# Expert selection of a product-key expert layer: keys by 0/1 matrix products, gated one-hots by VectorE alone, four result banks

## The chip, the cores and the metric

One core of a Trainium2 chip runs the whole program: TensorE (matmuls), VectorE (DVE), ScalarE (ACT), GpSimd (POOL) and SyncE (SP, which issues DMAs), with SBUF and PSUM between them. The metric is the device time of one execution in microseconds (us), the median of several runs.

## The reference, cut to what matters

The program computes two blocks of sequence mixers (a retention and a forgetting attention), a third mixer of stick-breaking attention and gated delta rule, and then an expert layer over 512 tokens of width 1024. Only the last is touched:

```python
q = einsum('bsd,de->bse', h, w_q).reshape(B, S, 8, 256)
s1 = einsum('bshd,hnd->bshn', q[..., :128], keys1)      # 128 keys per half
s2 = einsum('bshd,hnd->bshn', q[..., 128:], keys2)
v1, i1 = top_k(s1, 16);  v2, i2 = top_k(s2, 16)
cand = (v1[..., :, None] + v2[..., None, :]).reshape(B, S, 8, 256)
vals, c = top_k(cand, 16)
e1 = take_along_axis(i1, c // 16);  e2 = take_along_axis(i2, c % 16)
expert = e1 * 128 + e2                                  # one of 16384
gate = softmax(vals)
act = gelu(einsum('td,ted->te', hb, u_tab[expert]))
out = einsum('te,ted->td', gate * act, v_tab[expert])
```

Each token thus picks 8 heads x 16 = 128 experts, with a gate each.

## The kernel before, in words

The expert layer is the function `peer`. Tokens lie in four tiles of 128. The first three tiles (`nd` = 384 tokens) are computed densely: all 128 x 128 experts' products with a matrix of gates that is zero where a token did not pick an expert. That matrix, `gd`, is built in the kernel and kept in DRAM. The last tile gathers its experts' rows with indirect DMAs. Products that need float32 precision are three matmuls of split operands (`mm3`: high x high, low x high, high x low); `weights` loads 128 x 1024 weights, copies them to the high part on ScalarE (L206) and subtracts to the low part (L207) on the engine that `self.lo` names.

Five stretches follow each other.

- **Top-k.** For 8 heads and 2 halves: a projection into the bank `pacc` (24 matmuls of 512 columns), a copy (L1518), four score products into `psc` (L1523), a copy (L1525), and per tile `top16`, five VectorE operations (L1480 to L1484). After the second half come 64 additions of candidates on VectorE (`cd`, L1532) and `top16` of each sum. The projection's low weights are made on GpSimd.
- **Index.** `places` turns each candidate's number into two positions (small VectorE operations on 128 x 128). `keys` looks up the key at each position: a comparison of one-hots (L1576), a product with the indices (L1580), a reduction (L1567), all on VectorE, for a quarter of the heads and a half at a time. `gates` is the softmax (L1592 to L1597). The first tile is done here; the first 10 of the expert products `hidden(i)` stand here for TensorE to work at. One `hidden(i)` is 24 matmuls of 384 columns into `pst` and a copy (L1612): 384 tokens by the 128 experts of row i.
- **Gates.** `spread(t)` goes through 32 groups of 4 tokens for each of three tiles. Per group: two comparisons build the one-hots of the four tokens' 128 picks (`oo`, L1653, VectorE); ScalarE copies one into `o2` (L1657), GpSimd multiplies the other with the gates into `o1` (L1659), four products of 128 x 128 (L1635) go to one of two banks `ptr`, ScalarE copies the bank into a staging tile `big` (L1639), and after four groups a DMA writes it to `gd`. The keys of the next tile are searched in between, and 18 of the `hidden` stand between the groups (low weights on VectorE).
- **Tail.** Five `hidden`, the last ones of `lag` = 33, then transposes with the identity into the six banks `out`.
- **Rows.** For j = 0 to 127: the row's gates are loaded, multiplied with gelu of `hidden(j)` (L1750), split (L190, L191), 18 matmuls of 512 columns with the value weights go to `out`, then `hidden(j+33)`, and about 2.4 gathers of the last tile with their sums.

A tile scheduler keeps each engine's instructions in the order in which it places them by their dependencies; `add_manual_dep` adds an ordering by hand. Before `peer` the engines' instructions stand in the same order in both kernels.

Of the kernel before, what the change touches and what calls it, by code (L numbers as in the profile page):

```python
# [140 lines left out]
class Kern:  # L141
# [69 lines left out]
    def mm3(self, ps, lh, ll, rh, rl, start, stop, **kw):  # L211
        mm = self.nc.tensor.matmul
        mm(ps, lh, rh, start=start, stop=False, **kw)  # L213
        mm(ps, lh, rl, start=False, stop=False, **kw)  # L214
        mm(ps, ll, rh, start=False, stop=stop, **kw)  # L215

# [1269 lines left out]
    def peer(self):  # L1486
# [5 lines left out]
        with ExitStack() as cx:  # L1492
# [11 lines left out]
            first = self.pair()  # L1504
            io4 = tp.tile([128, 128, 4], BF, name="io4")
            nc.vector.tensor_copy(io4, io[:, :, None].to_broadcast([128, 128, 4]))

            self.lo = nc.gpsimd
            v = [tp.tile([128, 8, 2, 16], F32, name=f"tv{t}") for t in range(4)]
            ix = [tp.tile([128, 8, 2, 16], U32, name=f"tix{t}") for t in range(4)]  # L1510
            cv = [tp.tile([128, 8, 16], F32, name=f"cv{t}") for t in range(4)]
            ci = [tp.tile([128, 8, 16], U32, name=f"ci{t}") for t in range(4)]
            for h in range(8):
                for w in range(2):
# [11 lines left out]
                    for t in range(4):  # L1526
                        self.top16(sc[:, t], v[t][:, h, w], ix[t][:, h, w])
                for t in range(4):

                    cd = tp.tile([128, 112], F32, name="cd", bufs=2)  # L1530
                    for o, i0, ni, nj in ((0, 0, 4, 16), (64, 4, 12, 4)):
                        nc.vector.tensor_add(cd[:, o:o + ni * nj].rearrange("p (a b) -> p a b", a=ni),  # L1532
                                             v[t][:, h, 0, i0:i0 + ni, None].to_broadcast([128, ni, nj]),
                                             v[t][:, h, 1, None, :nj].to_broadcast([128, ni, nj]))
                    self.top16(cd, cv[t][:, h], ci[t][:, h])
            nosync = mybir.DependencyInfo(mybir.DependencyClass.NoSync, mybir.DependencyReason.SCHED_ONLY)
            sync = mybir.DependencyInfo(mybir.DependencyClass.Sync, mybir.DependencyReason.SCHED_ONLY)
            flat = lambda x: x.rearrange("p a b -> p (a b)")
            E, GT = {}, {}

            def places(t):

                ixf = tp.tile([128, 8, 2, 16], BF, name="ixf")
                nc.vector.tensor_copy(ixf, ix[t])
                f = []
                for sh in (4, 2):
                    u = tp.tile([128, 128], U32, name="ab")
                    nc.vector.tensor_scalar(u, flat(ci[t]), sh, None, op0=OP.logical_shift_right)
                    f.append(tp.tile([128, 128], BF, name=f"af{sh}"))
                    nc.vector.tensor_copy(f[-1], u)  # L1550
                a, b = f
                nc.vector.scalar_tensor_tensor(a, b, -12.0, a, op0=OP.add, op1=OP.max)
                o = tp.tile([128, 128], BF, name="af0")
                nc.vector.tensor_scalar(o, a, 4.0, 48.0, op0=OP.mult, op1=OP.add)
                nc.vector.scalar_tensor_tensor(o, a, 16.0, o, op0=OP.mult, op1=OP.min)
                nc.vector.tensor_copy(b, flat(ci[t]))
                nc.vector.tensor_sub(b, b, o)
                E[t] = [tp.tile([128, 128], F32, name=f"e{w}", bufs=2) for w in range(2)]
                return f, ixf

            def keys(t, f, ixf):

                todo = []

                def reduce(after):
                    e, oh = todo.pop(0)
                    i = nc.vector.tensor_reduce(e, oh.rearrange("p a e -> p e a"), axis=AX.X, op=OP.add)  # L1567
                    if after:
                        tc.add_manual_dep(i.ins, after, nosync, reason="behind the products")

                after = yield
                for w in range(2):
                    for q in range(4):
                        qs = slice(32 * q, 32 * q + 32)
                        oh = tp.tile([128, 16, 32], BF, name="oh", bufs=3)
                        nc.vector.tensor_tensor(oh.rearrange("p a (x y) -> p a x y", y=4),  # L1576
                                                f[w][:, None, qs].to_broadcast([128, 16, 32]).rearrange("p a (x y) -> p a x y", y=4),
                                                io4[:, :16, None, :].to_broadcast([128, 16, 8, 4]), op=OP.is_equal)
                        oh4 = oh.rearrange("p a (h k) -> p h a k", h=2)
                        nc.vector.tensor_tensor(oh4, oh4, ixf[:, 2 * q:2 * q + 2, w, :, None].to_broadcast([128, 2, 16, 16]),  # L1580
                                                op=OP.mult)
                        todo.append((E[t][w][:, qs], oh))
                        after = yield
                        if len(todo) == 2:
                            reduce(after)
                while todo:
                    reduce(after)
                    after = yield

            def gates(t):  # L1590
                gt = gate.rearrange("p (a b) -> p a b", a=8) if t == 3 else tp.tile([128, 8, 16], F32, name="gt", bufs=3)
                nc.vector.tensor_sub(gt, cv[t], cv[t][:, :, 0:1].to_broadcast([128, 8, 16]))  # L1592
                self.act(gt, gt, AF.Exp)
                sm = tp.tile([128, 8], F32, name="gsm")
                nc.vector.tensor_reduce(sm, gt, axis=AX.X, op=OP.add)
                nc.vector.reciprocal(sm, sm)
                nc.vector.tensor_mul(gt, gt, sm[:, :, None].to_broadcast([128, 8, 16]))  # L1597
                GT[t] = gt

            A1 = {}  # L1600

            def hidden(i):

                if i < lag:
                    self.lo = nc.gpsimd if i < 10 else nc.vector
                hi, lo = self.weights(A["peer_ut"][i], (8, 128))
                ps = self.ps("st", (128, nd))
                for k in range(8):
                    self.mm3(ps, hi[:, k], lo[:, k], self.hT[0][:, k, :nd], self.hT[1][:, k, :nd], k == 0, k == 7)
                a = A1[i] = pool.tile([128, nd], F32, name="a1", bufs=lag + 1)  # L1610
                if i < lag:
                    nc.scalar.activation(a, ps, AF.Copy)  # L1612
                else:
                    self.act(a, ps, AF.Gelu)

            ahead = iter(range(lag))

            NB = lag - 15

            def spread(t, other):  # L1620

                ps = self.ps("tr", (128, 3, 128))
                for i, src in enumerate((*E[t], flat(GT[t]))):
                    nc.tensor.transpose(ps[:, i], src, self.ident)
                eg = tp.tile([128, 2, 128], BF, name="egt", bufs=2)
                nc.scalar.activation(eg, ps[:, :2], AF.Copy)
                gt = tp.tile([128, 128], F32, name="ggt", bufs=2)
                nc.scalar.activation(gt, ps[:, 2], AF.Copy)
                todo = []

                def product(after):
                    g, o2, o1, stg = todo.pop(0)
                    ps = self.ps("tr", (128, 4, 128))
                    for i in range(4):
                        m = mm(ps[:, i], o2[:, i], o1[:, i], start=True, stop=True).ins  # L1635
                        if after and i == 0:
                            tc.add_manual_dep(m, after, nosync, reason="the gates are in")
                    q = g % 4
                    nc.scalar.activation(stg[:, :, 4 * q:4 * q + 4],  # L1639
                                         ps.rearrange("p t (a b) -> p a t b", a=16), AF.Copy)  # L1640
                    if q == 3:
                        n0 = t * 128 + g // 4 * 16
                        nc.sync.dma_start(gd[:, :, n0:n0 + 16].rearrange("g p t b -> p g t b"), stg)

                b4 = [128, 4, 128]
                for g in range(32):
                    if g % 4 == 0:
                        stg = tp.tile([128, 2048], F32, name="big", bufs=2).rearrange("p (g t b) -> p g t b", g=16, t=16)

                    oo = []  # L1650
# [10 lines left out]
                    if g % 2:  # L1661
                        other(after)
# [10 lines left out]
            for _ in keys(0, *first):  # L1673
                pass
# [127 lines left out]
```

## Time and profile before

| | us |
|---|---|
| runs | 3089.48, 3093.4, 3101.64 (median 3093.4) |
| the profiled execution | 3098.37 |
| its span, first to last instruction | 3096.5 |
| mean granted TensorE clock, of full speed | 0.985 |
| busy: TensorE, VectorE | 2913.6, 2183.2 |
| busy: ScalarE, GpSimd | 1310.0, 770.9 |
| where `peer`'s top-k begins | 1733.3 |

A row of the timeline gives the start in us, the duration, the engine, line and operation, the tiles written and read, and in brackets how long the engine sat idle before it and what ended that. Matmuls are pipelined: the distance between two starts, not a duration, is what one costs. "Busy" in the groups by line is the union of the instructions' times. Lines L214, L213 and L215 are the three matmuls of `mm3`, L207 is the subtraction that makes low weights.

### The profile page before, as it was taken

The numbers are of one execution on the slowest core, as the hardware profiler recorded it, in microseconds if no ns is written. First come the engines' busy times: TensorE is split into PE (matmuls) and PEld (weight loads), VectorE is DVE, ScalarE is ACT, GpSimd is POOL, SyncE is SP. The second block draws the span as 40 slices with busy tenths as digits, with TensorE's granted clock in tenths as the row PEclk, the third lists the DMA queues.
The fourth block names the chain that finished last, engine by engine and source line by source line (L and its number), as shares of the span: only waits on it lengthen the run. The fifth ranks groups of instructions, "written<-read, shape, count | busy, mean of one in ns | idle before, by whom it ended". The sixth has DMA issues, their size and how long they took to land.

```text
span 3096.5 us, 44003 instructions
## 1 busy us (share of the span) xinstructions
PE 2913.6 (94%) x16745; PEld 2546.9 (82%) x16745; DVE 2183.2 (71%) x4033; ACT 1310.0 (42%) x2279; POOL 770.9 (25%) x531
## 2 busy tenths in 40 slices
PE   6999999999999999999989987889999999999989
PEld 5887887888879887777777766779889998999867
DVE  5576456455575653798766899896877777888885
ACT  2222334455454543676244325664333333333323
POOL 0111011000010000111013334654555554333360
PEclk9999999999999999999999998999999999999999
DMA  5343222111112134434345223557888888888773
GB/s 210 130 170 124 81 82 70 62 48 49 69 65 80 42 106 140 145 115 173 96 157 199 76 74 99 160 159 281 323 311 303 295 292 302 301 305 301 282 267 131
DMA packets 201011, 516.67 MB, mean 167 GB/s; under 512 B 27104, under 2 KB 79456, under 8 KB 198496
## 3 DMA queue, kind: packets, MB, share of 16 engines
q1 hardware_dynamic: 163504, 379.36, 35.4%
q0 software_dynamic: 36864, 134.23, 11.8%
q8 instruction: 132, 2.16, 0.3%
q14 instruction: 79, 0.65, 0.1%
q10 hardware_dynamic: 432, 0.27, 0.0%
HBM read 462.15 MB, written 51.64 MB: 166 GB/s over the span
## 4 chain that ended last, share of the span: by engine, by line
PE 66%; DVE 17%; issue 5%; ACT 4%; POOL 4%; DMA 3%; SPq 0%; POOLq 0%; ACTq 0%; DVEq 0%
PE pacc L213 8%; PE pacc L214 8%; PE pacc L215 8%; PE out L214 5%; PE out L215 5%; PE out L213 5%; PE pst L215 4%; PE pst L213 4%; PE pst L214 4%; DVE oo L1653 2%; DVE wlo L207 2%; POOL g L1724 1%; ACT whi L206 1%; PE ppo L956 1%; POOL t L1659 1%
## 5 line engine op out<-in xcount | busy, mean ns | idle before, releaser
L207 DVE TENSOR_TENSOR wlo<-wraw,whi 128x1024 fp32r<-128x1024 f32 x320 | 403.1, 1260 | 252.2 <-ACT whi L206 250.7
L206 ACT ACTIVATE whi<-wraw 128x1024 fp32r<-128x1024 f32 x344 | 361.7, 1053 | 460.6 <-PE pacc L214 234.1
L213 PE MATMUL pst<-hTh,whi 128*128 128x384 f32 x1024 | 350.2, 342 | 30.2 <-ACT a L1612 30.2
L215 PE MATMUL pst<-hTh,wlo 128*128 128x384 f32 x1024 | 350.2, 342 | 0.0
L214 PE MATMUL pst<-hTl,whi 128*128 128x384 f32 x1024 | 349.9, 342 | 0.0
L213 PE MATMUL pacc<-whi,hTh 128*128 128x256 f32 x1216 | 341.1, 281 | 3.1 <-ACT whi L206 1.6
L214 PE MATMUL pacc<-wlo,hTh 128*128 128x256 f32 x1216 | 340.1, 280 | 0.0
L215 PE MATMUL pacc<-whi,hTl 128*128 128x256 f32 x1216 | 339.2, 279 | 0.0
L215 PE MATMUL out<-whi,wl 128*128 128x512 f32 x768 | 305.2, 397 | 7.4 <-DVE wl L191 7.4
L214 PE MATMUL out<-wlo,wh 128*128 128x512 f32 x768 | 305.2, 397 | 5.1 <-DVE wlo L207 5.0
L213 PE MATMUL out<-whi,wh 128*128 128x512 f32 x768 | 304.4, 397 | 0.1
L1724 POOL DMA_INDIRECT g<-in_peer_u_dram,ex x128 | 232.1, 1813 | 219.4 <-DVE w L1750 196.2
L206 ACT ACTIVATE whi<-vr 128x1024 fp32r<-128x1024 f32 x128 | 135.6, 1060 | 278.5 <-PE pst L214 255.7
L1724 POOL DMA_INDIRECT g<-in_peer_v_dram,ex x128 | 187.4, 1464 | 258.6 <-DVE w L1750 230.7
L213 PEld LDWEIGHTS pacc<-whi,hTh 128*128 128x128 f32 x1216 | 229.2, 189 | 4.9 <-ACT whi L206 1.8
L214 PEld LDWEIGHTS pacc<-wlo,hTh 128*128 128x128 f32 x1216 | 229.1, 188 | 0.5
L215 PEld LDWEIGHTS pacc<-whi,hTl 128*128 128x128 f32 x1216 | 228.8, 188 | 0.4
L213 PEld LDWEIGHTS pst<-hTh,whi 128*128 128x128 f32 x1024 | 196.1, 191 | 35.5 <-ACT a L1612 30.9
L213 PE MATMUL pacc<-hTh,whi 128*128 128x512 f32 x560 | 222.5, 397 | 1.6 <-ACT whi L206 1.0
L214 PE MATMUL pacc<-hTl,whi 128*128 128x512 f32 x560 | 222.8, 398 | 0.0
L215 PE MATMUL pacc<-hTh,wlo 128*128 128x512 f32 x560 | 222.5, 397 | 0.1
L190 ACT ACTIVATE wh<-w 128x384 fp32r<-128x384 f32 x128 | 67.2, 525 | 341.2 <-PE out L214 286.5
(635 smaller groups left out, 6898.6 us busy)
## 6 DMA issues: line engine op xcount, KB each, us to landing
wraw<-in_peer_ut_dram SPq DMA_DIRECT2D x128, 512.0 KB, 3.3
vr<-in_peer_v_dram SPq DMA_DIRECT2D x128, 512.0 KB, 5.0
gd<-big SPq DMA_DIRECT2D x24, 1024.0 KB, 5.3
gg<-gd SPq DMA_DIRECT2D x16, 1536.0 KB, 7.7
wraw<-in_mod_w_dram SPq DMA_DIRECT2D x32, 512.0 KB, 3.3
wraw<-in_ret_vg_dram SPq DMA_DIRECT2D x32, 512.0 KB, 3.6
wraw<-in_gdn_qkv_dram SPq DMA_DIRECT2D x24, 512.0 KB, 3.3
gd<-pk SPq DMA_DIRECT2D x8, 1280.0 KB, 4.6
```

Of the source, the lines that this page charges most:

```text
L190: nc.scalar.activation(hi, src, AF.Copy)
L206: self.nc.scalar.activation(hi, raw, AF.Copy)
L207: self.lo.tensor_tensor(lo, raw, hi.bitcast(F32), op=OP.subtract)
L213: mm(ps, lh, rh, start=start, stop=False, **kw)
L214: mm(ps, lh, rl, start=False, stop=False, **kw)
L215: mm(ps, ll, rh, start=False, stop=stop, **kw)
L956: m = mm(PO[h][:, 256 * g + c:256 * g + 256], v[a][:, j], pt[:, b, j, c:], start=first is None and g == 0, stop=j == 2 * g + 1 and a == 1, ...
L1653: after = nc.vector.tensor_tensor(oo[w], io4, eg[:, w, None, 4 * g:4 * g + 4].to_broadcast([128, 128, 4]), op=OP.is_equal).ins.name
L1659: nc.gpsimd.tensor_tensor(o1, turn(oo[0]), gt[:, 4 * g:4 * g + 4, None].to_broadcast(b4), op=OP.mult)
L1724: i = nc.gpsimd.indirect_dma_start(out=g, out_offset=None, in_=A["peer_u" if up else "peer_v"], in_offset=bass.IndirectOffsetOnAxis(ap=ex[ ...
```

## The change

In top-k, one `hidden` follows each head from the second on, the 64 additions `cd` go to GpSimd, and results go to two large tiles (`room`), part of which holds a 0/1 matrix `idk` that GpSimd builds before (L1513 of the new kernel). Gates and places are computed once for all four tiles. Keys are looked up by products: the indices and positions are transposed, and for each of 2 halves and 16 positions c, a product with `idk` (L1617) spreads index c of every head over the head's picks, one VectorE operation keeps it where the position is c (`hit`, L1619), and a product with the identity adds it up in PSUM (L1620). In the gate stretch the gated one-hot `o1` is written by four VectorE operations (L1660: equal to the key, times the gate, both per partition), without GpSimd; `o2` is as before. The result banks alternate over two pairs, `tr` and `acc`. 14 `hidden` stand between the groups, and four are ordered by hand behind the last gate product. All low weights of these stretches are made on GpSimd, and two value weights are loaded before the row loop.

```diff
+            room = [tp.tile([128, 2048], F32, name="big", bufs=2) for _ in range(2)]
+            idk = room[0][:, :1024].bitcast(BF).rearrange("p (c h k) -> p c h k", c=16, h=8)
+            nc.gpsimd.tensor_copy(idk, self.identb.rearrange("p (h a) -> p a h", a=16)[:, :, :, None].to_broadcast([128, 16, 8, 16]))
...
-                    cd = tp.tile([128, 112], F32, name="cd", bufs=2)
+                    cd = tp.tile([128, 112], F32, name="cd", bufs=4)
                     for o, i0, ni, nj in ((0, 0, 4, 16), (64, 4, 12, 4)):
-                        nc.vector.tensor_add(cd[:, o:o + ni * nj].rearrange("p (a b) -> p a b", a=ni),
+                        nc.gpsimd.tensor_tensor(cd[:, o:o + ni * nj].rearrange("p (a b) -> p a b", a=ni),
...
+                if h:
+                    for i in islice(ahead, 1):
+                        hidden(i)
...
+            for w in range(2):
+                tot = self.ps(("sc", "norm")[w])
+                for c in range(16):
+                    ps = self.ps("acc")
+                    mm(ps, idk[:, c], ixT[:, w], start=True, stop=True)
+                    hit = tp.tile([128, T], BF, name="hit", bufs=3)
+                    nc.vector.scalar_tensor_tensor(hit, fT[:, w], float(c), ps, op0=OP.is_equal, op1=OP.mult)
+                    mm(tot, self.identb, hit, start=c == 0, stop=c == 15)
+                    if c % 5 == 4:
+                        for i in islice(ahead, 1):
+                            hidden(i)
+                nc.scalar.activation(eg[w], tot, AF.Copy)
...
-                    oo = []
-                    for w in range(2):
-                        oo.append(tp.tile([128, 128, 4], BF, name="oo", bufs=4))
...
-                    nc.gpsimd.tensor_tensor(o1, turn(oo[0]), gt[:, 4 * g:4 * g + 4, None].to_broadcast(b4), op=OP.mult)
...
+            left = lag - 19
...
+                ps = self.ps(("tr", "acc")[g % 2], (128, 4, 128))
...
+            for g in range(96):
...
+                for i in range(4):
+                    n = 4 * g + i
+                    nc.vector.tensor_scalar(o1[:, i], iob, eg[0][:, n:n + 1], gtT[:, n:n + 1], op0=OP.is_equal, op1=OP.mult)
+                oo = tp.tile([128, 128, 4], BF, name="oo", bufs=2)
+                nc.vector.tensor_tensor(oo, io4, eg[1][:, None, gs].to_broadcast([128, 128, 4]), op=OP.is_equal)
...
+                for i in islice(ahead, (g + 1) * left // 96 - g * left // 96):
+                    hidden(i)
...
+            end = product()
...
             for i in ahead:
-                hidden(i)
+                hidden(i, end)
             self.lo = nc.vector
+            V = [self.weights(A["peer_v"][j * 128:j * 128 + 128], (2, 512)) for j in range(2)]
```

On TensorE, between the projections of the second and third head, this stood before (`psc`: scores, `pacc`: projection):

```order
L215 MATMUL pacc<-hTh,wlo 128x512
L213 MATMUL pacc<-hTh,whi 128x512
L1523 MATMUL psc<-kt,t_17017 128x128 x4
L214 MATMUL pacc<-hTl,whi 128x512
L215 MATMUL pacc<-hTh,wlo 128x512
L213 MATMUL pacc<-hTh,whi 128x512
```

and now, at the same place (`pst`: an expert product):

```order
L214 MATMUL pst<-hTl,whi 128x384
L215 MATMUL pst<-hTh,wlo 128x384
L1551 MATMUL psc<-kt,t_17006 128x128 x4
L213 MATMUL pst<-hTh,whi 128x384
L214 MATMUL pst<-hTl,whi 128x384
L215 MATMUL pst<-hTh,wlo 128x384
```

The expert product of 24 matmuls has moved in around the scores, ahead of the next projection.

On VectorE, a piece of the gate stretch before (the one-hots `oo` of each group, low weights, and the places and key reductions of the next tile):

```order
L1653 TENSOR_TENSOR oo<-io_16812,egt 128x512 x2
L207 TENSOR_TENSOR wlo<-wraw,whi 128x1024
L1653 TENSOR_TENSOR oo<-io_16812,egt 128x512 x2
L1567 TENSOR_REDUCE e_18441<-oh 128x32 x2
L1653 TENSOR_TENSOR oo<-io_16812,egt 128x512 x2
L207 TENSOR_TENSOR wlo<-wraw,whi 128x1024
L1544 CAST ixf<-tix_16820 128x256
```

and of the same stretch now (`t` is `o1`, four operations for a group):

```order
L1662 TENSOR_TENSOR oo<-io_16814,eg_18356 128x512 x2
L1660 TENSOR_SCALAR t_19204<-iob,eg_18355,gtT 128x128 x4
L1660 TENSOR_SCALAR t_19220<-iob,eg_18355,gtT 128x128 x4
L1662 TENSOR_TENSOR oo<-io_16814,eg_18356 128x512 x2
L1660 TENSOR_SCALAR t_19235<-iob,eg_18355,gtT 128x128 x4
```

One of each group's two one-hots has given way to four small operations, and nothing else stands between them.

On GpSimd, what follows the norm's last operation (`xh`) before:

```order
L516 TENSOR_TENSOR xh<-xT,R 128x256 x6
L207 TENSOR_TENSOR wlo<-wraw,whi 128x1024 x23
L1659 TENSOR_TENSOR t_18457<-oo,ggt 128x512
L1659 TENSOR_TENSOR t_18465<-oo,ggt 128x512
L1659 TENSOR_TENSOR t_18482<-oo,ggt 128x512
```

and at the end of top-k now:

```order
L207 TENSOR_TENSOR wlo<-wraw,whi 128x1024
L1560 TENSOR_TENSOR cd<-big 128x64 x2
L1560 TENSOR_TENSOR cd<-big 128x48
L207 TENSOR_TENSOR wlo<-wraw,whi 128x1024
L1592 COPY gate<-gt 128x128
L207 TENSOR_TENSOR wlo<-wraw,whi 128x1024 x22
L1707 DMA g<-in_peer_u_dram,ex 128x1024 x128
```

The multiplications are gone; additions stand between the low weights of top-k, and the low weights of all later expert products up to the row loop follow.

## Rows read from the trace of the kernel before

**Rows 1.** Windows: us, then PE, PEld, DVE, ACT, POOL busy, clock, DMA share, GB/s.

```profile
1733.30:1861.20 127.90, 109.91 (x560) 92.83 (x560) 125.96 (x830) 35.42 (x50) 42.44 (x18) 0.95 0.24 82
1861.20:1904.60 43.40, 31.16 (x159) 30.80 (x160) 37.97 (x73) 18.41 (x33) 12.80 (x5) 0.80 0.25 85
1904.60:2113.40 208.80, 177.75 (x1195) 167.50 (x1194) 185.31 (x297) 141.15 (x249) 129.83 (x96) 0.97 0.53 162
2113.40:2141.00 27.60, 27.50 (x180) 27.17 (x178) 7.42 (x9) 11.21 (x21) 1.31 (x1) 1.00 0.72 267
2141.00:3075.00 934.00, 921.45 (x4512) 818.03 (x4513) 740.14 (x854) 321.13 (x439) 418.19 (x255) 0.99 0.80 290
```

**Rows 2.** Timeline of TensorE in top-k: start, duration, engine, line, operation, tiles.

```profile
1759.99 0.39 PE L215 MATMUL pacc<-hTh,wlo 128*128 128x512 f32 x1
1760.22 0.39 PE L213 MATMUL pacc<-hTh,whi 128*128 128x512 f32 x1
...
1826.97 1.16 PE L1523 MATMUL psc<-kt,t 128*128 128x128 f32 x8
1827.88 0.42 PE L213 MATMUL pst<-hTh,whi 128*128 128x384 f32 x1
...
1836.29 0.34 PE L213 MATMUL pst<-hTh,whi 128*128 128x384 f32 x1
```

**Rows 3.** Groups by line: busy us, mean ns, idle before; top-k, last row whole span.

```profile
L1532 DVE TENSOR_TENSOR cd<-tv 128x64 f32<-128x64 f32 x32 | 14.6, 456 | 0.0
L1532 DVE TENSOR_TENSOR cd<-tv 128x48 f32<-128x48 f32 x32 | 6.1, 190 | 0.0
...
L516 POOL TENSOR_TENSOR xh<-xT,R 128x256 f32<-128x256 f32 x24 | 20.0, 843 | 23.9 <-ACT R L504 16.3 <-DVE hTl L191 4.5 <-DVE hTl L525 1.6
```

**Rows 4.** Windows of 10 us at the end of top-k, columns as in rows 1.

```profile
1850.00:1860.00 10.00, 0.00 (x0) 0.00 (x0) 9.96 (x71) 0.00 (x0) 0.00 (x0) 0.50 0.00 0
1860.00:1870.00 10.00, 5.84 (x22) 5.84 (x23) 10.00 (x31) 3.27 (x6) 4.97 (x2) 0.58 0.18 59
```

**Rows 5.** Timeline of GpSimd, then VectorE, at the start of the index stretch.

```profile
1863.81 4.97 POOL L207 TENSOR_TENSOR wlo<-wraw,whi 128x1024 fp32r<-128x1024 f32 x2 [25.46 <-ACT whi L206]
...
1864.12 2.40 DVE L1557 TENSOR_TENSOR af<-af,af 128x128 bf16<-128x128 bf16 x1
1866.45 2.88 DVE L1580 TENSOR_TENSOR oh<-oh,ixf 128x512 bf16<-128x512 bf16 x1
...
1870.55 0.68 DVE L1580 TENSOR_TENSOR oh<-oh,ixf 128x512 bf16<-128x512 bf16 x1
```

**Rows 6.** Lines L1653, L1659: duration min/median/max ns; then gate stretch groups by line.

```profile
L1653 DVE TENSOR_TENSOR oo<-io,egt x192: 402/415/1286, 1904.6 to 2108.5; 128x512 bf16<-128x512 bf16 x192
...
L1659 POOL TENSOR_TENSOR t<-oo,ggt x96: 1037/1100/3545, 1905.2 to 2108.8; 128x512 f32<-128x512 bf16 x96
...
L1635 PE MATMUL ptr<-t,t 128*128 128x128 f32 x767 | 102.2, 281 | 31.1 <-POOL t L1659 16.0 <-ACT big L1639 14.9
L207 DVE TENSOR_TENSOR wlo<-wraw,whi 128x1024 fp32r<-128x1024 f32 x19 | 26.6, 1397 | 15.1 <-ACT whi L206 15.0
```

**Rows 7.** VectorE's tensor_scalar: timeline rows, then lines L608 and L803 (min/median/max ns).

```profile
1618.77 0.48 DVE L1369 TENSOR_SCALAR xd<-xd,ss 128x128 f32<-128x128 f32 x2
...
1863.35 0.19 DVE L1554 TENSOR_SCALAR af<-af 128x128 bf16<-128x128 bf16 x1
...
L608 DVE TENSOR_SCALAR macc<-wraw,cact x4: 751/796/962, 66.8 to 280.3; 128x1024 f32<-128x1024 f32 x4
...
L803 DVE TENSOR_SCALAR ao<-ao,bmv,lnv x16: 517/541/548, 146.5 to 467.7; 128x512 f32<-128x512 f32 x16
```

**Rows 8.** Line L1372 on VectorE; timeline of TensorE at the row loop's start.

```profile
L1372 DVE SCALAR_TENSOR_TENSOR P<-pnorm,ogain,mTh x8: 742/751/754, 1569.5 to 1619.9; 128x512 f32<-128x512 f32 x8
...
2143.41 0.50 PE L214 MATMUL out<-wlo,wh 128*128 128x512 f32 x1 [1.48 <-DVE wlo L207]
```

**Rows 9.** Timeline of GpSimd before top-k.

```profile
1705.67 0.70 POOL L342 TENSOR_TENSOR rsy<-rsv,nhalf 128x2 f32<-128x2 f32 x1 [37.06 <-DVE rsv L493]
```

More of the change, by code (lines that the diff above doesn't have):

```diff
@@ new lines, in peer, with hidden @@
+            flat2 = lambda x: x.rearrange("p a b c -> p (a b c)")
+            A1 = {}
+            nosync = mybir.DependencyInfo(mybir.DependencyClass.NoSync, mybir.DependencyReason.SCHED_ONLY)
+            def hidden(i, after=None):
+                hi, lo = self.weights(A["peer_ut"][i], (8, 128))
+                ps = self.ps("st", (128, nd))
+                for k in range(8):
+                    m = self.mm3(ps, hi[:, k], lo[:, k], self.hT[0][:, k, :nd], self.hT[1][:, k, :nd], k == 0, k == 7)
+                    if after and k == 0:
+                        tc.add_manual_dep(m.ins, after, nosync, reason="behind the gates")
+                a = A1[i] = pool.tile([128, nd], F32, name="a1", bufs=lag + 1)
+                if i < lag:
+                    nc.scalar.activation(a, ps, AF.Copy)
+                else:
+                    self.act(a, ps, AF.Gelu)
@@ L1508, in peer @@
+            ahead = iter(range(lag))
             self.lo = nc.gpsimd
[L1509 to L1512, printed above, removed]
             for h in range(8):
@@ L1561, in keys @@
[L1561 to L1571, printed above, removed]
-                for w in range(2):
[L1573 to L1648, printed above, removed]
-                    oo = []
-                    for w in range(2):
-                        oo.append(tp.tile([128, 128, 4], BF, name="oo", bufs=4))
-                        after = nc.vector.tensor_tensor(oo[w], io4, eg[:, w, None, 4 * g:4 * g + 4].to_broadcast([128, 128, 4]),
-                                                        op=OP.is_equal).ins.name
-                    turn = lambda x: x.rearrange("p k t -> p t k")
-                    o2 = tp.tile(b4, F32, name="t2", bufs=6)
-                    nc.scalar.activation(o2, turn(oo[1]), AF.Copy)
-                    o1 = tp.tile(b4, F32, name="t2", bufs=6)
-                    nc.gpsimd.tensor_tensor(o1, turn(oo[0]), gt[:, 4 * g:4 * g + 4, None].to_broadcast(b4), op=OP.mult)
-                    todo.append((g, o2, o1, stg))
-                    if g % 2:
-                        other(after)
-                    n = 32 * t + g
-                    for i in islice(ahead, (n + 1) * NB // 96 - n * NB // 96):
-                        hidden(i)
-                    if len(todo) == 2:
-                        product(after)
-                product(None)
@@ L1670, in peer @@
-            first = places(0)
-            for i in islice(ahead, 10):
-                hidden(i)
-            for _ in keys(0, *first):
-                pass
-            for t in range(4):
-                gates(t)
-            for t in range(3):
-                k = keys(t + 1, *places(t + 1))
-                next(k)
-                done = []
-                def other(after):
-                    if not done:
-                        try:
-                            k.send(after)
-                        except StopIteration:
-                            done.append(1)
-                spread(t, other)
```

113 lines of the change are left out of this document (84 added, 29 removed).

## Prediction

> **What bounds the kernel now.** I read the table of windows first, cut at the stages of the expert layer [rows 1]. The last stage, the loop over 128 expert rows, takes 934 us with TensorE busy for 921.45; nothing in the change alters its work, so it moves as a block. What can move lies before it, in four stretches: the top-k stretch (127.9 us, VectorE 125.96, TensorE 109.91), the index stretch (43.4 us, VectorE 37.97, TensorE 31.16), the gate stretch (208.8 us, VectorE 185.31, TensorE 177.75, GpSimd 129.83) and the tail (27.6 us, TensorE only). So VectorE sets the first three, and TensorE follows within 18 to 31 us in the two long ones: a VectorE made faster hits TensorE soon.
>
> Second, what TensorE does meanwhile. Two 10 us windows at the end of top-k show it idle for ten and busy for 5.84 of the next ten, at granted clocks of 0.50 and 0.58, which is the lower of its two levels [rows 4]: the projections are over at 1827.88 [rows 2], the expert products that are ready run out, and VectorE still sorts.
>
> Third, why the gate stretch takes 208.8 us. Per group of four tokens VectorE builds two one-hots and GpSimd scales one of them; the medians are 0.415 us and 1.100 us [rows 6]. These don't overlap freely. Where GpSimd ran two subtractions from 1863.81 to 1868.78, two VectorE operations with two tensors in SBUF took 2.40 and 2.88 us; the second kind took 0.68 a few us later [rows 5]. Added in series, 96 x (2 x 0.415 + 1.10) is 185 us, and the low weights (19 operations, 26.6 us [rows 6]) bring it to 212, against 208.8 measured. The stretch is this exclusion.
>
> **The change, part by part.**
>
> *Top-k.* One expert product (24 matmuls) now follows each head but the first. By the order, TensorE issues 153 of their matmuls before its last score product, 144 more than before. They start 0.175 us apart (48 steps in 8.41 us) [rows 2], so they cost 25.2 us where TensorE has little spare time: the last scores come at 1827.9 + 25.2 = 1853. The 64 candidate additions leave VectorE, 14.6 + 6.1 = 20.7 us [rows 3], so it is no longer late: 96 sorts in 125.96 - 20.7 us are 1.10 each, and after a copy of some 0.6 us it sorts the last half-head (4.4), waits about 1.5 for GpSimd's additions and sorts four candidate sets (4.4): 1864, where the stretch ended at 1861.2. Thus it gains nothing itself; it takes over work that TensorE would do later, and fills the idle hole [rows 4]. What moves with it has room: its loads on SyncE's queue (DMA share 0.24), its copies on ScalarE (35.42 of 127.9 us) [rows 1]. One addition on GpSimd has no row. It lies between its 0.19 us on VectorE and the 0.843 of the 128x256 addition on GpSimd [rows 3]: 64 are 12 to 54 us. With 24 splits of about 2.45 us [rows 5], 59 us, GpSimd has 71 to 113 us of work in 130, so it holds at either end, though an addition may queue behind a split. I take a value near the smaller end, since the tiles are a quarter of that size or less. The 0/1 matrix is built by GpSimd in a gap of 37.06 us [rows 9], and costs nothing unless it takes longer than that.
>
> *Index.* The gates and places are computed once for all four tiles, in about 14 VectorE operations on 512 elements (0.3 to 0.75 us each), with transposes behind them: the first lookup product at about 1871. Then TensorE has 162 expert matmuls x 0.175 = 28.4, 64 products of 512 columns at 0.23 (the pitch of the projection's 512 columns [rows 2]) = 14.7, and transposes, 2.3. VectorE's 32 gated compares are like the row at 0.751 us [rows 8], 24 us, beside them. The first gate product thus comes at 1871 + 45.4, about 1917, against 1904.6: **+12.4**. Bounds: 1910 if the expert matmuls also cover the wait up to 1871, 1930 if each lookup waits in turn for VectorE, or if TensorE runs part of it at the lower clock.
>
> *Gate stretch.* All key searches leave VectorE here, and GpSimd's 96 multiplications go. New per group are four tensor_scalar operations (128x128, bfloat16 in, float32 out, two per-partition operands) and one one-hot. No row shows that form. Nearest: one operand, float32, 128 wide, two in 0.48 us, a pitch of 0.20 (each lasts 0.28 and overlaps the next by 0.08); immediates, bfloat16, 0.19 long and so a pitch of 0.11; two operands, 512 wide, 0.541 long, a pitch of 0.46; and 1024 wide with one operand, 0.796 [rows 7]. From 128 to 1024 with one operand adds 0.52 us, 0.58 ns an element; the 384 elements between the wide two-operand row and ours are worth 0.22, which leaves 0.24. I take **0.25**, a little for the change of type; the bounds are 0.11 and 0.46. A one-hot has a pitch of 0.415 - 0.08 = 0.335. So VectorE needs 96 x (4 x 0.25 + 0.335) = 128 us. Each of 14 splits on GpSimd (2.4 us) stops it, if what [rows 5] show holds for these operations too: 33.6 more, 162, with a start-up **163**. TensorE needs 96 groups at 1.07 (102.2 us in all [rows 6]) and 318 expert matmuls, 55.7: 158 by busy time, and some 150 (an estimate) where groups follow each other closely, since the 1.07 has the ramp of groups that stand alone in it. ScalarE is below its 141.15 [rows 1]. So VectorE ends last, by little: 208.8 to 163, **-45.8**. Four result banks instead of two then cost and gain nothing. The last gate product comes at about 2080, against 2113.4.
>
> [...]
>
> *Tail.* Four expert products stand behind the last gate product, before it five: 24 x 0.175 = **-4.2**. Two value weights are loaded ahead, and hold two of the three buffers through which the next hidden weights must pass. The stall of 1.48 us at the loop's start [rows 8] should go, and one of 1 to 2.4 us come (a split as long as GpSimd's or VectorE's): **+1.5** for what I can't place.
>
> Sum: +12.4 - 45.8 - 4.2 + 1.5 = **-36.1**. The profiled execution took 3098.37 us, so 3062.3; it lies 5.0 above the median of 3093.4, so **3057**.
>
> **Rivals.**
>
> (a) *TensorE becomes the bound.* If the tensor_scalars run at the lower pitch, or GpSimd's splits don't stop them, VectorE needs 96 x (4 x 0.11 + 0.335) + 33.6 = 108, or 128 + 8; TensorE's 150 to 158 sets the stretch. With 152: 11 less than the forecast, **3046**. For it: the operations have one tensor input, and the stretched rows have two. Against: two operands per partition, and the wide row's 0.541.
>
> [...]
>
> (b) *The gain is smaller: stages interlock.* An expert product waits for GpSimd's split, which waits for VectorE, which is shut out by the next; or the lookup runs at the lower clock. With 180 us for the gate stretch, or 1930 for its start, the sum is -19 to -25: **3073**. For it: VectorE and TensorE are within 15 us of one another, so each wait shows. Against: the splits are issued well ahead, three buffers deep.
>
> (c) *Slower: the two-operand tensor_scalar is dear.* At 0.46 the stretch takes 96 x (4 x 0.46 + 0.335) + 33.6 = 242 us, +79 against the forecast: **3136**. It decides from a pitch of about 0.345, where the stretch takes 198.5 and all gains are used up. Against: it needs a cost that does not shrink with the tile, while three quarters of the elements went.
>
> (d) *The change doesn't do what it says:* TensorE, with the same 792 expert matmuls and some 80 products more, bounds the whole, and the idle time only moves to another place: within 10 us of before, **3088**.
>
> **How the numbers follow.** Forecast 0.52 (3050 to 3066), (a) 0.18, (b) 0.17, (c) 0.07, (d) 0.06. A measurement of this kernel can tell about 0.5%, 15.5 us, from no change. Faster by more than that: forecast, (a) and half of (b), 0.78. Within: the rest of (b) and (d), 0.14. Slower: 0.08, with a little of what is unforeseen. The range leaves out (c) and the outermost of (a): 3038 to 3092.
>
> **What would show it.** Right: the last score product near 1853 and no 10 us window with TensorE at zero; the first gate product at 1910 to 1925; the tensor_scalars 0.24 to 0.28 apart and in places stretched to over 2 us beside GpSimd's splits; the gate stretch 160 to 170 us with VectorE busy nearly all of it; the row loop at 934. Wrong: tensor_scalars at 0.11 to 0.15 or never stretched (a), TensorE waiting for GpSimd's splits in the gate stretch (b), a pitch above 0.345 (c), or a loop over rows that is longer than 934 by more than 3.

## The result, and the profile after

The changed kernel took 3059.93 us in the median of six runs (3055.21 to 3080.10), the kernel before 3095.56 in as many: a ratio of 0.9897, interval 0.988 to 0.9914, some 32 us. Forecast were 3057 us and a range of 3038 to 3092. The profiled execution took 3056.85 us, with a span of 3055.1.

The windows of the changed kernel, cut at its own stretches (columns as in rows 1, and in that order: top-k, index, gates, tail, row loop):

```profile
1733.30:1863.40 130.10, 130.10 (x678) 113.23 (x678) 111.23 (x769) 43.85 (x62) 72.44 (x88) 1.00 0.30 101
1863.40:1913.60 50.20, 45.49 (x246) 33.96 (x249) 32.66 (x56) 22.74 (x38) 17.02 (x8) 1.00 0.22 74
1913.60:2081.40 167.80, 154.25 (x1089) 143.34 (x1087) 157.00 (x474) 130.49 (x231) 32.38 (x14) 1.00 0.65 188
2081.40:2104.80 23.40, 23.33 (x156) 23.11 (x156) 4.96 (x4) 9.87 (x17) 4.26 (x2) 1.00 0.68 211
2104.80:3033.60 928.80, 919.54 (x4512) 814.14 (x4512) 739.18 (x855) 320.00 (x439) 402.82 (x256) 1.00 0.81 294
```

Against [rows 1]: TensorE is busy through all of top-k, the granted clock is 1.00 in all five windows, and the gate stretch is 41 us shorter.

Where comparisons go to single microseconds, one pair of marks serves for all kernels: the first and last score product, the first and last product of the gate stretch, the last identity product of the tail, and the end of the span.

| from mark to mark, us | before | before, profiled again | after |
|---|---|---|---|
| span's start to first score product | 1733.3 | 1748.2 | 1733.1 |
| to last score product | 94.5 | 94.7 | 119.7 |
| first score to first gate product | 173.0 | 172.9 | 180.5 |
| gate stretch, first to last product | 207.1 | 207.0 | 167.7 |
| tail, to last identity product | 27.2 | 27.2 | 23.2 |
| rest, to the span's end | 955.9 | 946.7 | 950.6 |

The stretches between score products and tail repeat within 0.3 us in the kernel before; what precedes them scattered by 15 us and the row loop by 9. The change is worth +7.5 - 39.4 - 4.0 = -35.9 us in the stretches that repeat; the medians differ by 35.6.

VectorE's timeline in the gate stretch of the changed kernel, and with it GpSimd's at that time (start, duration, engine, line, operation, tiles, count):

```profile
1916.01 2.13 DVE L1660 TENSOR_SCALAR t<-iob,eg,gtT 128x128 f32<-128x128 bf16 x8
1918.06 0.75 DVE L1662 TENSOR_TENSOR oo<-io,eg 128x512 bf16<-128x512 bf16 x2
1918.73 3.18 DVE L1660 TENSOR_SCALAR t<-iob,eg,gtT 128x128 f32<-128x128 bf16 x4
...
1918.79 2.52 POOL L207 TENSOR_TENSOR wlo<-wraw,whi 128x1024 fp32r<-128x1024 f32 x1 [6.46 <-ACT whi L206]
```

Eight tensor_scalars last 2.13 us; one alone is 0.336, so the pitch is (2.13 - 0.336) / 7 = 0.256 us. Four should last 1.10. With a GpSimd split (the subtraction that makes low weights) over them they last 3.18: the split took 2.08 us from VectorE. Who waits on TensorE in the same stretch (waits in us, times, longest):

```profile
PE ptr L1641 <- ACT t L1664: 4.4, 8, 0.7
PE pacc L1641 <- ACT t L1664: 4.1, 7, 0.7
PE pacc L1641 <- DVE t L1660: 2.6, 4, 0.7
PE ptr L1641 <- DVE t L1660: 2.1, 3, 0.7
```

These 13.2 us are nearly all of TensorE's idle time there (167.80 - 154.25 = 13.5). They come in pieces of at most 0.7 us, for `t`, the one-hots that VectorE wrote or that ScalarE copied from VectorE's. VectorE is idle for 10.8 us. For 6.8 of them it waits for TensorE to free the tiles `t` and for ScalarE to free `oo`; the other 4 lie behind its last operation:

```profile
DVE t L1660 <- PE ptr L1641: 2.4, 5, 0.6
DVE oo L1662 <- ACT t L1664: 2.4, 6, 0.4
DVE t L1660 <- PE pacc L1641: 2.0, 4, 0.6
```

### The profile page after: what moved, and what is told of

Read it like the earlier page. It is cut to its first block, busy times and chain, and to the rows that moved or that the text cites. A ratio compares the mean times of both kernels' runs of the same rounds, so it can differ in the third digit from the quotient of the medians.

```text
span 3055.1 us, 44135 instructions
## 1 busy us (share of the span) xinstructions
PE 2916.9 (95%) x16816; PEld 2536.2 (83%) x16820; DVE 2133.6 (70%) x4130; ACT 1309.9 (43%) x2275; POOL 697.4 (23%) x524
## 3 DMA queue, kind: packets, MB, share of 16 engines
q1 hardware_dynamic: 163504, 379.36, 36.1%
## 4 chain that ended last, share of the span: by engine, by line
PE 72%; DVE 14%; issue 4%; ACT 4%; POOL 4%; DMA 2%; SPq 0%; ACTq 0%; POOLq 0%; DVEq 0%
PE pacc L213 10%; PE pacc L214 9%; PE pacc L215 9%; PE pst L215 5%; PE pst L214 5%; PE pst L213 5%; PE out L214 5%; PE out L215 5%; PE out L213 5%; DVE t L1660 3%; POOL g L1707 2%; DVE wlo L207 1%; PE ppo L957 1%; DVE cv L1217 1%; ACT whi L206 1%
## 5 line engine op out<-in xcount | busy, mean ns | idle before, releaser
L207 DVE TENSOR_TENSOR wlo<-wraw,whi 128x1024 fp32r<-128x1024 f32 x299 | 375.9, 1258 | 252.7 <-ACT whi L206 251.3
L1707 POOL DMA_INDIRECT g<-in_peer_v_dram,ex x128 | 176.2, 1376 | 255.4 <-DVE w L1733 231.0
```

The costliest lines, as they stand in the source:

```text
L207: self.lo.tensor_tensor(lo, raw, hi.bitcast(F32), op=OP.subtract)
L1707: i = nc.gpsimd.indirect_dma_start(out=g, out_offset=None, in_=A["peer_u" if up else "peer_v"], in_offset=bass.IndirectOffsetOnAxis(ap=ex[ ...
```

## The experiments

After the first, each is an edit of the changed kernel, or of one of its variants. Each was profiled once; a time of the whole kernel is given only for the two that were timed four times.

**The kernel before, profiled again.**

> The kernel before, profiled a second time, for how far the stretches scatter. If the row loop's 955.5 us against 950.3 in the changed kernel is the change's doing, it is 954 to 957 again; if it is the scatter of executions, it lies anywhere between 948 and 958, while top-k, index and gate stretches repeat within 1 us.

Its gate stretch and its row loop (columns as in rows 1):

```profile
1921.10:2128.10 207.00, 174.66 (x1187) 164.77 (x1188) 181.34 (x294) 140.19 (x247) 132.17 (x95) 0.98 0.53 162
2155.70:3080.50 924.80, 920.04 (x4512) 816.62 (x4513) 740.52 (x854) 320.98 (x439) 409.66 (x255) 1.00 0.82 293
```

The loop took 924.8 us for the 934.00 of [rows 1], by the same program, a little more than was expected of scatter. So the 5.3 us that the row loop gained in the changed kernel's profile are not shown to be the change's.

**Is VectorE the bound of the gate stretch?** A fifth tensor_scalar per group:

```diff
+                sp = tp.tile([128, 128], F32, name="spare")
+                nc.vector.tensor_scalar(sp, iob, eg[0][:, n:n + 1], gtT[:, n:n + 1], op0=OP.is_equal, op1=OP.mult)
                 oo = tp.tile([128, 128, 4], BF, name="oo", bufs=2)
```

> A fifth tensor_scalar per group, written to a spare tile that nothing reads: 96 more of them. Theory (VectorE sets the gate stretch, at a pitch of 0.256 us): +96 x 0.256 = 24.6 us, the stretch 167.8 to about 192, VectorE without gaps. Rival (TensorE with 154.25 us busy, or the waits between engines, set it and VectorE only follows): the 10.8 us in which VectorE was not busy take up part, +14 or less.

```profile
1923.40:2101.30 177.90, 156.80 (x1087) 141.90 (x1087) 175.31 (x540) 131.16 (x232) 34.31 (x14) 0.99 0.62 179
```

The stretch grew by 10.2 us. But nothing reads the spare tile, and not all 96 operations fell into the stretch:

```profile
L1662 DVE TENSOR_SCALAR spare<-iob,eg,gtT x96: 328/336/2442, 1900.4 to 2097.2; 128x128 f32<-128x128 bf16 x96
```

29 of them ran before the first gate product (1923.4), among the lookups, and that product came 184.3 us after the first score product, for 180.5 in the changed kernel. So 67 operations, 17.2 us at the pitch of 0.256, lengthened the stretch by 10.2, and all 96, 24.6 us, the way to the last gate product by 14.0. VectorE went from 10.8 us of idle time in the stretch to 2.6, and waits for nothing there any more. The theory expected +24.6 and no gaps, the rival +14 or less: VectorE nearly sets the stretch of the changed kernel. A part of what is added fills its waits, the rest lengthens the way.

**Do GpSimd's splits cost what the rows say?** The low weights of this stretch on VectorE:

```diff
             STG = []
+            self.lo = nc.vector
             for g in range(96):
...
             end = product()
+            self.lo = nc.gpsimd
```

> The low weights of the 14 expert products in the gate stretch on VectorE instead of GpSimd, all else as in the changed kernel. Theory (a GpSimd split shuts VectorE out for some 2.1 us of its 2.45): 14 x (2.08 - 1.13) = 13 us less on VectorE, the stretch falls from 167.8 towards TensorE's 154, to 156 to 160, and TensorE's waits for o1 and o2 mostly go. Rival (the long operations are only the profile's, or VectorE doesn't set the stretch): VectorE gets 14 x 1.13 = 16 us more work, the stretch stays or grows up to 184.

The window of the gate stretch, VectorE's timeline around one split, and all of TensorE's waits for this stretch:

```profile
1918.70:2068.40 149.70, 147.90 (x1087) 140.14 (x1087) 146.30 (x484) 129.22 (x231) 5.29 (x3) 1.00 0.73 211
```

```profile
1964.51 2.13 DVE L1661 TENSOR_SCALAR t<-iob,eg,gtT 128x128 f32<-128x128 bf16 x8
1966.56 0.75 DVE L1663 TENSOR_TENSOR oo<-io,eg 128x512 bf16<-128x512 bf16 x2
1967.23 1.21 DVE L207 TENSOR_TENSOR wlo<-wraw,whi 128x1024 fp32r<-128x1024 f32 x1
1968.37 2.13 DVE L1661 TENSOR_SCALAR t<-iob,eg,gtT 128x128 f32<-128x128 bf16 x8
```

```profile
PE pacc L1641 <- ACT t L1665: 0.7, 2, 0.4
PE ptr L1641 <- DVE t L1661: 0.5, 1, 0.5
PE ptr L1641 <- ACT t L1665: 0.2, 1, 0.2
```

The stretch fell to 149.7 us, 18.0 less and below the 156 expected, with one more kind of work on VectorE. TensorE is busy for 147.9 of it, so it sets the stretch now. The whole kernel took 3045.17 us (ratio to before 0.9834, interval 0.9802 to 0.9865, the changed kernel's being 0.988 to 0.9914): the fastest version of this study. The windows show 14 operations on GpSimd in the changed kernel and 3 here: those 3 are splits of the expert products behind the stretch. So 11 fewer GpSimd splits gave 18.0 us, 1.64 us each.

**How much of the gain is the gating?** The old gating in the new kernel: two comparisons, and GpSimd's multiplication (with it, the keys `eg[0]` become bfloat16 and `oo` gets four buffers, as before):

```diff
-                for i in range(4):
-                    n = 4 * g + i
-                    nc.vector.tensor_scalar(o1[:, i], iob, eg[0][:, n:n + 1], gtT[:, n:n + 1], op0=OP.is_equal, op1=OP.mult)
+                oa = tp.tile([128, 128, 4], BF, name="oo", bufs=4)
+                nc.vector.tensor_tensor(oa, io4, eg[0][:, None, gs].to_broadcast([128, 128, 4]), op=OP.is_equal)
+                nc.gpsimd.tensor_tensor(o1, oa.rearrange("p k t -> p t k"), gtT[:, gs, None].to_broadcast(b4), op=OP.mult)
```

> The gate stretch's one-hot gating undone alone: two comparisons on VectorE and the multiplication on GpSimd again, all else as in the changed kernel. Theory (the two exclude each other, in series 2 x 0.335 + 1.10 to 1.16 = about 1.8 us a group, and 14 splits of 2.45 in the same lock): 96 x 1.8 + 34 = 207, the stretch 200 to 210, near the 208.8 of before, so that the gating carries the gate term. Rival (the gain came from the key searches that left VectorE, or the two more banks): the stretch stays below 185.

Its window, and three rows each of VectorE and GpSimd:

```profile
1928.00:2108.70 180.70, 154.57 (x1089) 144.77 (x1087) 134.14 (x189) 131.26 (x231) 133.03 (x109) 0.99 0.60 175
```

```profile
1960.27 1.27 DVE L1659 TENSOR_TENSOR oo<-io,eg 128x512 bf16<-128x512 bf16 x1
1961.46 0.41 DVE L1662 TENSOR_TENSOR oo<-io,eg 128x512 bf16<-128x512 bf16 x1
1961.80 1.28 DVE L1659 TENSOR_TENSOR oo<-io,eg 128x512 bf16<-128x512 bf16 x1
...
1960.18 1.07 POOL L1660 TENSOR_TENSOR t<-oo,gtT 128x512 f32<-128x512 bf16 x1 [0.45 <-DVE oo L1659]
1961.68 1.10 POOL L1660 TENSOR_TENSOR t<-oo,gtT 128x512 f32<-128x512 bf16 x1 [0.43 <-DVE oo L1659]
1963.24 1.08 POOL L1660 TENSOR_TENSOR t<-oo,gtT 128x512 f32<-128x512 bf16 x1 [0.46 <-DVE oo L1659]
```

180.7 us, 13.0 more than the changed kernel, below the 200 expected and on the rival's side of 185: the theory of the gate term falls. The exclusion is there (L1659 takes 1.27 us where a comparison alone takes 0.41), but a group's period is 1961.80 - 1960.27 = 1.53 us, not 1.8: the second comparison of a group starts in the gap between two multiplications (at 1961.46; they leave 1961.25 to 1961.68 free) and is not lengthened (0.41). The kernel before has the same period, 1978.50 - 1976.98 = 1.52 us, where nothing else stands between its groups:

```profile
1976.98 1.10 POOL L1659 TENSOR_TENSOR t<-oo,ggt 128x512 f32<-128x512 bf16 x1 [0.43 <-DVE oo L1653]
1978.50 1.09 POOL L1659 TENSOR_TENSOR t<-oo,ggt 128x512 f32<-128x512 bf16 x1 [0.42 <-DVE oo L1653]
```

With it, the theory's own sum gives 96 x 1.53 + 14 x 2.4 = 180.5. In the new kernel the gating is worth 13.0 us, a third of the gain of 39.4.

A new theory was formed: the rest is due to the key searches. They were put back into that kernel, 24 of them with unused results:

```diff
+                if g % 4 == 1:
+                    oh = tp.tile([128, T], BF, name="hit", bufs=3).rearrange("p (a e) -> p a e", a=16)
+                    nc.vector.tensor_tensor(oh.rearrange("p a (x y) -> p a x y", y=4), ..., op=OP.is_equal)
+                    oh4 = oh.rearrange("p a (h k) -> p h a k", h=2)
+                    nc.vector.tensor_tensor(oh4, oh4, ..., op=OP.mult)
+                    en = tp.tile([128, 32], F32, name="en", bufs=1)
+                    nc.vector.tensor_reduce(en, oh.rearrange("p a e -> p e a"), axis=AX.X, op=OP.add)
```

> As the run with the gating back on GpSimd (gate stretch 180.7 us), and every fourth group one key search as the kernel before made them in this stretch (compare, product, reduction on VectorE, 24 of each, results unused). New theory, after that run: before, the gate stretch was 208.8 because the searches were added to the alternation of VectorE and GpSimd; compare and product (0.34 + 0.60) cannot run beside GpSimd, the reduction (0.96) partly can: 24 x 0.94 = 23 to 24 x 1.9 = 46 us more, 203 to 226. Rival (the two added banks and the four expert products that left the stretch explain the rest): the searches fit beside GpSimd's work, 180 to 189.

```profile
1925.10:2135.60 210.50, 166.57 (x1083) 156.79 (x1083) 180.88 (x257) 131.22 (x231) 141.73 (x109) 0.92 0.51 148
```

29.8 us more, 210.5, as the theory expected. They ran in the first 120 us:

```profile
1925.10:2045.10 120.00, 88.99 (x536) 84.13 (x536) 116.87 (x167) 65.92 (x116) 75.45 (x55) 0.86 0.43 123
```

VectorE is busy there for 116.9 us of 120 and sets the pace. The granted clock was 0.86 there and TensorE was idle for 31 us; with VectorE this full, the lower clock can explain little (an estimate). So with old gating and searches the new kernel has a gate stretch about as long as the old one's 207.1, and the searches are the larger part of the difference.

That they cost 29.8 us in the kernel before, too, is not shown. There the 19 low weights were on VectorE, which stood idle for 15.0 us before them, waiting for ScalarE's copies [rows 6], and GpSimd's multiplications waited 22.0 us for TensorE to free their tiles:

```profile
L1659 POOL TENSOR_TENSOR t<-oo,ggt 128x512 f32<-128x512 bf16 x96 | 129.8, 1360 | 85.6 <-DVE oo L1653 63.6 <-PE ptr L1635 22.0
```

In the run with the searches put back, GpSimd's multiplications waited only 1.6 us for TensorE. It has four banks for two, four expert products fewer, and its low weights on GpSimd; what each of these is worth together with the old gating was not run.

**Do four banks matter?** With two:

```diff
-                ps = self.ps(("tr", "acc")[g % 2], (128, 4, 128))
+                ps = self.ps("tr", (128, 4, 128))
```

> The changed kernel with two result banks in the gate stretch instead of four. Theory (VectorE ends last there, results wait for no bank): the stretch stays at 167.7 within 1.5 us. Rival (the 14.9 us in which TensorE waited for ScalarE's copies before come back): 175 to 183.

The stretch took 169.0 us, 1.3 more: TensorE's wait for ScalarE's copy out of the bank is there again, and mostly takes the place of other waits:

```profile
PE ptr L1641 <- ACT t L1664: 7.5, 8, 1.0
PE ptr L1641 <- ACT big L1646: 5.1, 7, 1.0
```

The same with the splits on VectorE:

> Splits of the gate stretch on VectorE and two result banks instead of four. Theory (with four banks TensorE is busy 147.9 of 149.7 us there; with two it waits for ScalarE's copies as it did for 5.1 us in the run with two banks alone): 153 to 158. Rival (banks never matter here): 149.7 within 1 us.

```profile
1918.20:2068.20 150.00, 147.91 (x1086) 140.05 (x1086) 146.23 (x484) 129.34 (x231) 5.26 (x3) 1.00 0.73 210
```

150.0 for 149.7: that theory fell too. In the changed kernel the added banks are worth about nothing, with or without the splits' stops; with the old gating this was not run.

**What closed the hole at the end of top-k?** The seven expert products behind top-k again, alone:

```diff
-                if h:
-                    for i in islice(ahead, 1):
-                        hidden(i)
...
-            for i in islice(ahead, 2):
+            for i in islice(ahead, 9):
                 hidden(i)
```

> The seven expert products are taken out of top-k and stand behind it again (nine there), all else as changed. Last score product 25 us earlier (after 94.7 us instead of 119.7). Theory (their place in top-k fills time in which TensorE would stand idle): VectorE, without the candidate additions, sorts until about 1845, two expert products fit into the two banks meanwhile, then TensorE waits for ScalarE, whose copies are behind the exponential of the gates: a hole of 5 to 12 us, and the first gate product that much later than 180.5 us after the first score product. Rival (the order does not matter, the same work fits behind): within 2 us.

The additions on VectorE again, alone:

```diff
-                        nc.gpsimd.tensor_tensor(cd[:, o:o + ni * nj].rearrange("p (a b) -> p a b", a=ni),
+                        nc.vector.tensor_tensor(cd[:, o:o + ni * nj].rearrange("p (a b) -> p a b", a=ni),
```

> The 64 candidate additions back on VectorE, all else as changed: 20.7 us more work there in top-k. Theory (TensorE sets top-k, VectorE has 19 us to spare): first gate product 0 to 3 us later. Rival (the additions' move is what made room): 10 us or more later.

And both:

> Both edits of top-k undone at once: the additions on VectorE, the seven expert products behind top-k. Undone alone they cost 1.9 and 3.7 us. Theory (either alone nearly closes TensorE's hole at the end of top-k: additions elsewhere let VectorE end sooner, expert products keep TensorE busy until it ends): together the hole of the kernel before is back, last scores at 94.7 us after the first, VectorE until 126 to 130 us after, two expert products in between: first gate product 12 to 25 us later than 180.5. Rival (they are independent): 5.6 us later, 184 to 188.

The lines of the score products and of the first gate products (durations min/median/max in ns, then first to last start), for the changed kernel, then without the weaving, with the additions on VectorE, and with both:

```profile
L1551 PE MATMUL psc<-kt,t x128: 275/275/377, 1733.1 to 1852.8; 128*128 128x128 f32 x128
...
L1641 PE MATMUL ptr<-t,t x384: 270/275/377, 1913.6 to 2080.4; 128*128 128x128 f32 x192
```

```profile
L1551 PE MATMUL psc<-kt,t x128: 275/275/377, 1744.8 to 1839.5; 128*128 128x128 f32 x128
...
L1638 PE MATMUL ptr<-t,t x384: 270/275/377, 1929.0 to 2096.0; 128*128 128x128 f32 x192
```

```profile
L1551 PE MATMUL psc<-kt,t x128: 275/275/377, 1736.4 to 1856.2; 128*128 128x128 f32 x128
...
L1641 PE MATMUL ptr<-t,t x384: 270/275/378, 1918.9 to 2085.9; 128*128 128x128 f32 x192
```

```profile
L1551 PE MATMUL psc<-kt,t x128: 275/275/378, 1737.2 to 1831.9; 128*128 128x128 f32 x128
...
L1638 PE MATMUL ptr<-t,t x384: 270/275/377, 1936.6 to 2103.3; 128*128 128x128 f32 x192
```

From first score to first gate product: 180.5, 184.2, 182.5 and 199.4 us. Alone the edits cost 3.7 (less than the 5 to 12 expected) and 2.0; together 18.9. The waits of TensorE without the weaving, and without both, show it: the same wait, 3.1 and 21.3 us long.

```profile
PE pst L213 <- ACT a L1535: 3.1, 1, 3.1
```

```profile
PE pst L213 <- ACT a L1535: 21.3, 1, 21.3
```

`L1535` is the copy of an expert product out of its bank. On ScalarE it stands behind the gates' exponential, and that waits for `gt`, which VectorE makes after its last sorts; here is the exponential with both edits undone, and TensorE's same wait in the kernel before:

```profile
1866.55 0.63 ACT L184 ACTIVATE gt<-gt 128x512 f32<-128x512 f32 x1 [26.23 <-DVE gt L1567]
...
1864.16 0.69 PE L213 MATMUL pst<-hTh,whi 128*128 128x384 f32 x1 [20.95 <-ACT a L1612]
```

So this is the hole of the kernel before, 20.95 us there and 21.3 here. Either edit closes it almost entirely.

**Can TensorE's idle time be filled?** 17 expert products between the groups, one behind (`left = lag - 16` for `lag - 19`); first with the splits on GpSimd, then on VectorE.

> The changed kernel with 17 expert products between the gate groups instead of 14, and one behind instead of four. Theory (TensorE has 13.5 us idle in the gate stretch, VectorE and GpSimd's lock end last there): 3 x 24 x 0.174 = 12.5 us leave the tail (23.2 to 10.7), the stretch grows by what three more splits take from VectorE, 3 x 2.08 = 6 us, to 174; net -6. Rival (TensorE sets it already): the stretch takes them in full, 180, net 0.

> Splits of the gate stretch on VectorE, and 17 expert products between the groups, one behind. Theory (TensorE is at its floor in this stretch, only 1.8 us idle): the stretch grows by the full 12.5 us that the tail loses, 162 and 10.7, net 0 to -1.8 against splits alone. Rival (some idle time is still hidden in the busy figure): net -4 or more.

Gate stretch and tail took 181.0 and 10.7 us, for 167.7 and 23.2: 0.8 longer together, where 6 less was expected. With the splits on VectorE they took 162.4 and 10.6, for 149.7 and 23.2: as expected, nothing gained (3051.66 us, ratio to before 0.9855, interval 0.982 to 0.989, which overlaps that of the version without). The windows of the two gate stretches:

```profile
1927.20:2108.20 181.00, 165.38 (x1160) 156.81 (x1159) 162.99 (x475) 135.55 (x240) 36.64 (x15) 1.00 0.63 183
```

```profile
1918.20:2080.60 162.40, 160.78 (x1161) 153.07 (x1159) 149.78 (x489) 134.10 (x240) 2.45 (x1) 1.00 0.70 204
```

So the idle time of TensorE in the changed kernel is not spare room for these products: it was 13.5 us and is 15.6 with three more of them. With the splits on VectorE it is 1.8 and 1.6: it comes with the splits on GpSimd. Moving those is worth 181.0 - 162.4 = 18.6 us here, and was worth 18.0 before.

## Why the prediction was right, step by step

- **Top-k.** 25.2 us later to the last score product were forecast and 25.2 measured; top-k was to gain nothing itself, and its end, 1863.4, is where it was put (1864). That it "fills the idle hole" is right: with both edits of top-k undone the hole is back (18.9 us). But either alone would have closed most of it, which the working did not see. Of the "two levels" of the clock: in windows of 1 us over the kernel before, the granted clock is 1.00 in 2982 of 3096, 0.50 in 82 and between the two in 32, never below; the 0.58 of [rows 4] is a mean of both.
- **Additions on GpSimd.** Bounds 0.19 to 0.843 us; the 64 have a median of 0.280. GpSimd was busy for 72.44 us of top-k, near the lower end that was chosen. The 0/1 matrix took 2.356 us in the gap of [rows 9].
- **Index.** The first lookup was put at 1871 and the first gate product at 1917; they came at 1869.3 and 1913.6. The sum's +12.4 was counted from 1904.6, VectorE's first one-hot; by the products' own mark (1906.3) it was +10.7, and +7.5 was measured. The clock stayed at 1.00, the gated compares took 0.686 us for the 0.751 of [rows 8].
- **Gate stretch.** The form that no row showed was priced well: pitch 0.256 for 0.25, in between rows that gave 0.11 and 0.46. So was TensorE's part, "some 150 (an estimate)": 147.9 with 11 of the splits away from GpSimd. The length was not far off, 167.7 for 163, but the account behind it has two weak steps. "VectorE ends last, by little" holds nearly (its last operation ends some 4 us before the last product), but the sum of its work, 162, leaves out that it waits for the others: it was busy for 157.0 us and idle for 10.8. And the reading of the kernel before, "the stretch is this exclusion", 185 us of alternation plus 26.6 of low weights, is wrong: the alternation's period is 1.52 us, 146 us for 96 groups; beyond the low weights the rest was filled by the key searches (29.8 us when put back into the new kernel) and by waits such as the 15.0 us before the low weights, in shares that stay open. The prediction had the searches leave VectorE without a price. Its sum of 212 happened to end near 208.8, so agreement with the total did not show that the account was right; the new stretch came out because it was added up anew, and not from this reading.
- **The splits.** That a GpSimd split stops VectorE's tensor_scalars held: at 1918.73 four take 3.18 us beside one for 1.10 without, and all 13 splits that lie beside tensor_scalars in this stretch lengthen them by 2.07 to 2.13 us, against the 2.4 assumed (the 14th comes behind VectorE's last operation). Moving the splits away gave 18.0 us back. Rival (a), in which the splits don't stop them or the pitch is lower, fell.
- **Interlocking (b)** is there, within the forecast's range: the splits' stops show on TensorE as 13.2 us of short waits (1.4 with the splits on VectorE), which three more expert products did not fill.
- **Tail and loop.** -4.2 forecast, -4.0 measured. The +1.5 for the loop's start cannot be seen in a loop that scatters by 9 us.

By marks the forecast was +10.7 - 44.1 - 4.2 + 1.5 = -36.1 (the same sum with the 1.7 us between the two marks moved); measured +7.5 - 39.4 - 4.0, with the loop left out. An index stretch too dear by 3.2 us and a gate stretch too cheap by 4.7 nearly cancelled: that the totals agree within 1 us is luck.

## What to carry to other kernels

Work taken from VectorE and given to GpSimd is not gone where VectorE's operations take longer beside it: here a 2.4 us operation on GpSimd held VectorE's tensor_scalars up by 2.08 us and cost the stretch some 1.6 us more than the same operation on VectorE (1.21 us there), and the idle time that this left on TensorE, 13.5 us, was not filled by three more expert products (15.6 with them). When a stretch's length agrees with a sum, take one term out on the chip before building on it: here the named exclusion was a third of the gain, and the removal that had no price cost more than twice as much when it was put back. Look also at where the scheduler puts an added operation that nothing reads: 29 of 96 fell outside the stretch that they were to test. And undo paired edits both singly and together: here each alone looked worth 2 to 4 us, the pair 19.

## What the runs showed of the hardware that was not expected

- Tensor_scalars with one tensor operand in SBUF and two per-partition scalars, bfloat16 in and float32 out, were held up by a GpSimd subtraction about as much as an operation with two tensors was: four took 3.18 us beside a split for 1.10 without, 2.08 more; the product with two tensors of [rows 5] took 2.88 for 0.68, 2.20 more.
- GpSimd's additions of 128 x 48 and 128 x 64 elements between strided operands took 0.259 to 0.307 us here, about a third of the 0.843 of a 128 x 256 addition [rows 3].
- The first score product came anywhere from 1733.1 to 1748.2 us after the start of the span in these profiles, 1733.3 and 1748.2 in the two of the kernel before, while that kernel's stretches of 27 to 207 us after it repeated within 0.3 us. Where the 15 us arise is open.
